# An earlier weight order, a later sum of squares and a second issuer of outputs in a three-layer kernel

## The chip, the cores and the metric

The kernel runs on one core of a Trainium2 chip. The metric is the device time of one execution in microseconds (us), given as the median of several runs. The core has five engines that matter here: TensorE (PE, with its weight loads shown apart as PEld), VectorE (DVE), ScalarE (ACT), GpSimd (POOL) and SyncE (SP), which mostly issues transfers. Each engine takes its instructions in the order in which the program holds them, and semaphores make one wait for another.

## The reference

512 tokens of 1024 features go through three layers in fp32. Each layer starts with an rms norm, whose scale per token is `rsqrt(mean(x*x) + 1e-6)`. The change touches the start of the first layer and the very end.

```python
def rmsnorm(x, g):
    return x * lax.rsqrt(jnp.mean(x * x, axis=-1, keepdims=True) + EPS) * g

def even_mixer(h, w_in, sink, w_pool, pool_scale, w_out):
    z = h @ w_in                                   # q, k, v and u side by side
    q, k, v, u = jnp.split(z, [...], axis=-1)
    q, k = rope(q), rope(k)
    ya = windowed_gqa(q, k, v, sink)               # 8 heads, 2 key heads, |i-j| <= 128
    yb = multiscale_pool(u, w_pool, pool_scale)    # centred means over 2, 4, 8, 16 tokens
    return jnp.concatenate([ya, yb], axis=-1) @ w_out

x = x + even_mixer(rmsnorm(x, g0), ...);  x = x + sq_relu_mlp(rmsnorm(x, g1), ...)
x = x + odd_mixer(rmsnorm(x, g2), ...);   x = x + sq_relu_mlp(rmsnorm(x, g3), ...)
...                                        # a third mixer and a gated embedding
return rmsnorm(x, norm_final)
```

## The kernel before

Every matrix product is computed as three products of two-part numbers: an operand is split into a high part of fewer bits and a low remainder, and hi·wh, hi·wl and lo·wh are added up in PSUM. So each piece of a weight (`wr`, as it comes from memory) needs a `wh` (a rounding copy) and a `wl` (`wr` minus `wh`) before TensorE can use it, and each of the 8 chunks of the transposed activations `x` (128 features by 512 tokens) needs a `hi` and a `lo`. In the first norm the gain is folded into `hi` and `lo`; the scale per token (`rb`) is multiplied in after the first matrix product, so that product can start before the norm is known.

The first tile of the program is the weight unit `ein2`, 8 pieces of 128x256 (k = 0 to 7), by the 8 chunks of `x`: for each k six matmuls of 512 columns, 48 in all, into two PSUM tiles. Then come the units `ein0`, `ein1` and so on in pieces of 128x1024. From the eight chunks also come the squares for the norm: `sq<-x` squares a chunk, `sq<-sq,sq` adds two partial sums, and when all eight are in one tile four matmuls by a column of ones (`tr<-onec,sq`) sum them over features. From there the chain is `ms` (DVE), `pw` (POOL, the power), `tr<-cst,pw` (PE, which spreads the scale over partitions), `rb<-tr` (a DVE copy), and then the rotary tables `cst<-cst,rb`. Every q and k head needs these tables: a raw product is copied to `zs`, turned on PE (`tr<-zs`), combined by `ra` and `rbb`, split into `q` or `kh` and `kl`, and only then do the scores `sc`, their maxima `mx`, the probabilities `p`, their turned halves `ph` and `pl` and the products `av` follow, head after head. Between these stand matmuls of other units that need no norm; they are what keeps TensorE at work while the other engines do the attention.

Where an instruction stands, and on which engine, is set while the program is built: a planner keeps a clock (`fl.now`) and an estimate of when each engine is free (`_Engine.cost`), steps a list of generators, and lets `first` choose the engine that would be done first. Constants of that choice stand in the table `_TUNE`, one row for each phase: `gw` is added to the estimate of POOL for weight splits, `gt` for adds, `gc` for copies, so a larger number keeps that work off POOL. A generator that waits for another (`waitc`) is passed over until the other is planned. So a small edit in the front re-orders everything up to the point at which the plans fall together again. For the first layer's mixer the row is "a". The outputs are written at the end by `outputs`: a PSUM tile is scaled by ACT or DVE (again by `first`) and written to memory by a DMA that SP issues.

Of the kernel before, what the change touches and what calls it, by code (L numbers as in the profile page):

```python
# [18 lines left out]
P = 128  # L19
T = 512  # L20
# [220 lines left out]
def _constants():  # L241
# [40 lines left out]
    for dl in (4, 16):  # L282
# [16 lines left out]


_TUNE = {
    "a": dict(slack=2, gc=0.3, gt=-0.6, gw=-0.5, low=1, lat=0.1, wide=1, mm=4, sc=2, tr=5, av=2, ahead=3,
              streams=3, share=0.1),
    "b": dict(slack=0.5, gc=0.4, gt=0, gw=0, low=4, lat=0.15, wide=2, mm=4, sc=4, tr=4, av=2),
# [63 lines left out]
class _Flow:  # L368
# [12 lines left out]
    def go(self, gen, low=False):  # L381
        t = _Task(gen, low)
        t.due = self.now + 0.1
        self.tasks.append(t)
        return t
# [103 lines left out]
def tile_hybrid(ctx: ExitStack, tc: tile.TileContext, wt, xT, pT, prm_d, cst_d, out):  # L489
    nc = tc.nc  # L490
# [3 lines left out]
    fl = _Flow()  # L494
    go = fl.go
    V, S, G = (_Engine(fl, e, k) for e, k in ((nc.vector, "V"), (nc.scalar, "S"), (nc.gpsimd, "G")))
# [13 lines left out]
    def uid(s):  # L510
        cnt[0] += 1
        return f"{s}{cnt[0]}"

    def blk(name="b", dt=F32, n=T):
        return bp.tile([P, TB], dt, tag="b", bufs=NB, name=uid(name))[:, 0:n]
# [17 lines left out]
    def take(tag):  # L533
        while (t := bank(tag)) is None:
            yield
        return t
# [6 lines left out]
    def give(tag):  # L543
        banks.append(max(fl.now, fl.last) + 0.1)
        held[tag] -= 1

    def wait(*tasks):
        for t in tasks:
            while not t.done:
                yield  # L550

    def waitc(*tasks):
        for t in tasks:
            while not t.done:
                yield 0.1
# [15 lines left out]
    def first(*engines):  # L571

        return min(engines, key=lambda e: max(e[0].free, fl.now) + e[1])[0]
# [28 lines left out]
    units, order = {}, []  # L602
# [160 lines left out]
    x, x_at = [], []  # L763
    for c in range(NC):

        x.append(blk("x"))
        (nc.scalar if c == 0 else nc.sync).dma_start(x[c], xT[:, c, :])
        wl["dma"] = max(wl["dma"], fl.now) + 0.73
        x_at.append(wl["dma"] + 2.0)
        order[c // 4].load()  # L770
        if c == 0:
            nc.sync.dma_start(prm, prm_d)
    cst = cons.tile([P, NKEEP], F32, name="cst")
# [11 lines left out]
    def PR(name, i=0, n=1):  # L785
        o, w = _PO[name]
        return prm[:, o + i:o + i + n]
# [55 lines left out]
    def mm3(ps, w, c, a, start, stop, m=P, bw=P, cs=slice(0, T), keep=False):  # L843

        us = 0.216 * (cs.stop - cs.start) / T
        wh, wlo = yield from w.at(c, bw, keep)
        mm(ps, wh[:, :m], a.hi[:, cs], start, False, us)
        mm(ps, wlo[:, :m], a.hi[:, cs], False, False, us)
        mm(ps, wh[:, :m], a.lo[:, cs], False, stop, us)
        yield  # L850
# [86 lines left out]
    def v_stack(z):  # L937

        ps = yield from takec("tr")
        for b in range(NQ):  # L940
            tr(ps[:, b * P:(b + 1) * P], z[:, b * P:(b + 1) * P], ident)
        r = []
        yield
        for i in range(2):
            v = blk("v", F32R).rearrange("p (b h t e) -> p b h t e", b=2, h=2, t=2)
            src = ps[:, 256 * i:256 * i + 256].rearrange("p (b h e) -> p b h e", b=2, h=2)
            copy(v[:, :, :, 0, :], src)
            r.append((v, src))
        yield
        for v, src in r:  # L950
            V.tensor_sub(v[:, :, :, 1, :], src, f(v[:, :, :, 0, :]))
        give("tr")
        yield
        return lambda kb, h: r[kb // 2][0][:, kb % 2, h, :, :]
# [12 lines left out]
    def k_stacks(z, dst, i=0):  # L967

        ks = [(blk("kh", F32R), blk("kl", F32R)) for _ in range(2)]
        for r0, (kh, kl) in zip((0, 64), ks):  # L970
            copy(kh[r0:r0 + 64], z[r0:r0 + 64])
            copy(kh[64 - r0:128 - r0], z[r0:r0 + 64])
        yield
        for r0, (kh, kl) in zip((0, 64), ks):
            V.tensor_sub(kl[r0:r0 + 64], z[r0:r0 + 64], f(kh[r0:r0 + 64]))
            V.tensor_sub(kl[64 - r0:128 - r0], z[r0:r0 + 64], f(kh[r0:r0 + 64]))
        yield
        dst[i], dst[i + 1] = ks
# [162 lines left out]
    def attend(jobs, ahead=2, streams=1):  # L1141

        n = [0, 0]

        def scores():
            for ready, score, _ in jobs:
                while n[0] - n[1] >= ahead or (ready is not None and not ready()):
                    yield
                yield from score()
                n[0] += 1  # L1150

        def applies(k):
            for i in range(k, len(jobs), streams):
                while n[0] <= i:
                    yield
                yield from jobs[i][2]()
                n[1] += 1

        return _both(*[applies(k) for k in range(streams)], scores())
# [69 lines left out]
    h = acts()  # L1229

    def start(c):
        while fl.now < x_at[c]:
            yield 0.1
        yield from split_to(h[c], x[c], PR("e_norm", c))

    def sums():
        for c in range(NC):
            yield from waitc(h[c])
            go(ss.add(x[c]))

    for c in range(NC):
        go(start(c))
    go(sums())
    r_t, rb = rms(ss)
    cosr, sinr = C("cos64"), C("sin64")
# [22 lines left out]
    def rope64(ps, then):  # L1268

        zs = blk("zs")  # L1270
        S.activation(zs, ps, AF.Copy)
        give("mm")
        yield
        yield from waitc(rp)
        ps2 = yield from takec("tr")
        mm(ps2, C("perm"), zs, True, True, 0.86)
        a, b_ = blk("ra"), blk("rbb")
        tt(ALU.mult, a, zs, cosr)
        yield
        V.tensor_mul(b_, ps2, sinr)  # L1280
        give("tr")
        tt(ALU.add, a, a, b_)
        yield
        yield from then(a)
# [12 lines left out]
    def kv_blocks():  # L1297
        w = weights("ein2")
        kps = yield from take("mm")
        ps = yield from take("mm")  # L1300
        for k in range(NC):
            yield from wait(h[k])
            for b, o in enumerate((kps, ps)):
                yield from mm3(o, w, (2 * k + b) * P, h[k], k == 0, k == NC - 1)
        go(rope64(kps, lambda z: k_stacks(z, ks)))

        def vchain(ps=ps):
            yield from waitc(rb)
            z = blk("vz")
            V.tensor_mul(z, ps, rb.t)  # L1310
            give("mm")
            yield
            v0.append((yield from v_stack(z)))

        go(vchain())
# [57 lines left out]
    def store(hd, base, post=None):  # L1373

        def done(po):
            i = hd // 2
            if i not in yz:
                yz[i] = [blk("ya"), 0]
            y = yz[i][0]
            yield from combine(po, y[64 * (hd % 2):64 * (hd % 2) + 64])  # L1380
            yz[i][1] += 1
            if yz[i][1] == 2:
                del yz[i]
                if post is not None:
                    yield from post(i, y)
                yield from split_to(yhl[base + i], y)
        return done

    def job0(hd):
        st = {}  # L1390

        def score():
            g = hd // 4
            q = qs[hd]
            st["h"] = Head([(q, ks[g][0]), (q, ks[g][1])], band3, band3_masks, lambda kb: v0[0](kb, g),
                           SC64, nsink=nsink[:, hd:hd + 1], sink=PR("sink", hd))
            return st["h"].score()

        return (lambda: hd in qs and 1 in ks and v0 and nmask.done, score,
                lambda: st["h"].apply(done=store(hd, 4)))  # L1400

    fl.phase("a")
    fl.run(kv_blocks(), None)
    fl.run(attend([job0(i) for i in range(8)], fl.ahead, fl.streams), fill, fl.share)
    ss = SumSq(NC)
    h, then = next_norm(lambda c: PR("n_mlp0", c), (ss, None))
# [98 lines left out]
    h = h2  # L1505
# [276 lines left out]
    h, then = next_norm(lambda c: PR("n_mlp1", c), (ss, None))  # L1782
# [15 lines left out]
    h = h2  # L1798
# [73 lines left out]
    gt = cons.tile([P, 18, NQ], F32, name="gt")  # L1872
# [480 lines left out]
    def outputs(t, b, j, r, tag):  # L2353

        yield from waitc(dense)
        ps = yield from takec(tag)
        for i in range(4):
            z = xg[NC * t + 4 * j + i]
            yield from waitc(z)
            tr(ps[:, i * P:(i + 1) * P], z.t[:, 256 * t + b * P:256 * t + (b + 1) * P], ident)  # L2360
        yield
        yield from waitc(r)
        o = blk("o")
        if first((S, 0.53), (V, 0.6)) is S:
            S.activation(o, ps, AF.Copy, scale=r.t[:, b:b + 1])
        else:
            V.tensor_scalar(o, ps, r.t[:, b:b + 1], None, op0=ALU.mult)
        give(tag)
        q = 256 * t + P * b
        nc.sync.dma_start(out[q:q + P, T * j:T * j + T], o)  # L2370
        yield

    fl.phase("e")
# [13 lines left out]
    h = h2  # L2387
# [26 lines left out]
```

## Time and profile before

| what | value |
|---|---|
| median of 3 runs | 1486.02 us (1485.08 to 1486.47) |
| the profiled execution, its own time | 1481.19 us |
| its span, first to last instruction | 1479.4 us |
| mean granted TensorE clock | 0.993 |
| PE busy | 1450.2 us, 98% of the span |
| DVE busy | 906.4 us, 61% |
| ACT busy | 639.5 us, 43% |
| POOL busy | 328.3 us, 22% |

The durations of the section on rows belong to the profiled execution, which ran 4.8 us below the median. In the rows, a name such as `wl<-wr,wh` tells the tile written and the tiles read, with buffer numbers left out; `128x512` is partitions by elements. What stands in square brackets is how long the engine had been idle before the row, and what ended that wait. The mixer that this change re-orders lies in the first 160 us of the span. Matmuls of 512 columns follow each other every 0.23 us although each shows about 0.39, since they are pipelined.

### The profile page before, as it was taken

What the parts mean: (1) busy time and instruction counts of PE and PEld (TensorE: products, weight loads), DVE (VectorE), ACT (ScalarE), POOL (GpSimd) and SP (SyncE); (2) the same over time, 40 slices, a digit from 0 to 9 for tenths busy, and PEclk for the clock granted to TensorE, in tenths of its full rate; (3) what the DMA queues carried; (4) which work ended last, traced back from release to release, by engine and by line L of the source; (5) the groups of instructions that cost most, each with busy time, mean ns of one, the idle gap of its engine ahead of it and who ended that gap; (6) DMA issues with size and microseconds to landing.
All of it is one profiled execution on the core that took longest, in us unless ns stands there. A gap on an engine that the chain in (4) does not pass through costs nothing.

```text
span 1479.4 us, 18899 instructions
## 1 busy us (share of the span) xinstructions
PE 1450.2 (98%) x6789; PEld 1175.9 (79%) x6789; DVE 906.4 (61%) x1414; ACT 639.5 (43%) x1175; POOL 328.3 (22%) x307
## 2 busy tenths in 40 slices
PE   8999999999999999799999999999999999999998
PEld 5777878888888887688888888888887788888787
DVE  7896865646434458987675665756755566536413
ACT  5684433323223345477343433334521575324623
POOL 5441220202102026542120210202110000110332
PEclk9999999999999999899999999999999999999999
DMA  6113688898333363331599999999855323346352
GB/s 220 44 43 100 209 276 284 284 290 283 108 100 101 141 221 130 127 129 72 188 312 332 334 325 331 320 334 320 305 204 201 114 86 115 114 174 216 109 196 88
DMA packets 118317, 291.44 MB, mean 197 GB/s; under 512 B 13136, under 2 KB 14672, under 8 KB 118224
## 3 DMA queue, kind: packets, MB, share of 16 engines
q1 hardware_dynamic: 118080, 289.98, 57.7%
q8 instruction: 53, 0.87, 0.2%
q14 instruction: 40, 0.33, 0.1%
q10 hardware_dynamic: 144, 0.26, 0.1%
HBM read 205.26 MB, written 84.93 MB: 196 GB/s over the span
## 4 chain that ended last, share of the span: by engine, by line
PE 90%; DVE 5%; DMA 2%; ACT 1%; issue 1%; POOL 0%; SPq 0%; POOLq 0%; DVEq 0%; ACTq 0%
PE mm L561 78%; PE sc L561 4%; PE tr L565 3%; PE av L561 3%; DVE sg L363 2%; PE tr L561 1%; DMA kr<-in_wt_dram 1%; DVE lo L363 1%; DVE wl L363 1%; DMA pin<-in_pT_dram 0%; DMA x<-in_xT_dram 0%; ACT wh L363 0%; DMA wk<-khi 0%; ACT sg L363 0%; POOL ma L363 0%
## 5 line engine op out<-in xcount | busy, mean ns | idle before, releaser
L561 PE MATMUL mm<-hi,wh 128*128 128x512 f32 (+1 forms) x1276 | 508.4, 398 | 0.8 <-POOL wh L363 0.5
L561 PE MATMUL mm<-hi,wl 128*128 128x512 f32 (+1 forms) x1276 | 502.1, 393 | 4.8 <-DVE wl L363 2.7
L561 PE MATMUL mm<-lo,wh 128*128 128x512 f32 (+1 forms) x1276 | 500.2, 392 | 0.3 <-POOL lo L363 0.3
L561 PEld LDWEIGHTS mm<-hi,wl 128*128 128x128 f32 x1276 | 241.0, 189 | 56.1 <-DVE wl L363 4.2
L561 PEld LDWEIGHTS mm<-lo,wh 128*128 128x128 f32 x1276 | 240.9, 189 | 55.3 <-POOL lo L363 0.8
L561 PEld LDWEIGHTS mm<-hi,wh 128*128 128x128 f32 x1276 | 241.2, 189 | 53.0 <-issue 1.1
L363 ACT ACTIVATE khi<-kr 128x512 fp32r<-128x512 f32 x120 | 75.9, 632 | 304.6 <-DMA kr<-in_wt_dram 298.3
L561 PE MATMUL mm<-ul,wh 128*128 128x512 f32 x512 | 201.6, 394 | 0.3 <-DVE ul L363 0.3
L561 PE MATMUL mm<-uh,wh 128*128 128x512 f32 x512 | 201.6, 394 | 0.0
L561 PE MATMUL mm<-uh,wl 128*128 128x512 f32 x512 | 201.5, 394 | 0.0
L363 DVE TENSOR_TENSOR wl<-wr,wh 128x1024 fp32r<-128x1024 f32 (+1 forms) x145 | 182.9, 1262 | 6.2 <-ACT wh L363 5.6
L363 DVE TENSOR_TENSOR klo<-kr,khi 128x512 fp32r<-128x512 f32 x150 | 121.4, 810 | 81.8 <-ACT khi L363 73.1
L363 ACT ACTIVATE wh<-wr 128x1024 fp32r<-128x1024 f32 (+1 forms) x147 | 148.8, 1013 | 47.6 <-PE mm L561 34.4
L363 DVE TENSOR_TENSOR x<-x,mm 128x512 f32<-128x512 f32 x112 | 76.8, 686 | 147.1 <-PE mm L561 143.7
L363 POOL TENSOR_TENSOR ma<-ma 128x512 f32<-128x512 f32 x62 | 86.6, 1397 | 279.3 <-ACT uh L363 237.6
L561 PEld LDWEIGHTS mm<-ul,wh 128*128 128x128 f32 x512 | 96.1, 188 | 23.8 <-DVE ul L363 1.3
L561 PEld LDWEIGHTS mm<-uh,wl 128*128 128x128 f32 x512 | 96.2, 188 | 22.3
L561 PEld LDWEIGHTS mm<-uh,wh 128*128 128x128 f32 x512 | 96.1, 188 | 22.3
L363 ACT ACTIVATE p<-sc,nm 128x512 f32<-128x512 f32 (+3 forms) x136 | 75.3, 557 | 27.8 <-DVE nm L363 24.8
L363 POOL TENSOR_SCALAR khi<-kr 128x512 fp32r<-128x512 f32 x30 | 29.6, 986 | 248.1 <-DMA kr<-in_wt_dram 225.8
L363 DVE TENSOR_TENSOR pl<-tr,ph 128x512 fp32r<-128x512 f32 (+2 forms) x108 | 66.3, 624 | 27.9 <-ACT ph L363 27.1
L363 DVE SCALAR_TENSOR_TENSOR ma<-mm,rb 128x512 f32<-128x512 f32 x64 | 44.1, 690 | 59.0 <-PE mm L561 58.9
(293 smaller groups left out, 1633.4 us busy)
## 6 DMA issues: line engine op xcount, KB each, us to landing
wr<-in_wt_dram SPq DMA_DIRECT2D x144, 512.0 KB, 5.2
kr<-in_wt_dram SPq DMA_DIRECT2D x150, 256.0 KB, 5.8
wk<-khi SPq DMA_DIRECT2D x150, 256.0 KB, 5.9
wk<-klo SPq DMA_DIRECT2D x150, 256.0 KB, 5.7
wh<-wk SPq DMA_DIRECT2D x74, 512.0 KB, 3.3
wl<-wk SPq DMA_DIRECT2D x74, 512.0 KB, 4.2
x<-xs SPq DMA_DIRECT2D x16, 256.0 KB, 5.0
cst<-in_cst_dram SPq DMA_DIRECT2D x8, 256.0 KB, 5.1
```

The costliest lines, as they stand in the source:

```text
L363: return fn(*a, **k)
L561: PE.matmul(o, l, r, start=start, stop=stop, skip_group_check=True)
L565: PE.transpose(o, i, idn)
```

## The change

There are four edits. The weight piece of `ein2` is asked for ahead of the chunk of `x` of the same k, not behind it. A new phase "s", with 3 us put on POOL for weight splits and adds, holds while the first tile is planned; phase "a" begins behind it. The generator of the sums (`sums`) starts only when all eight splits of `x` are planned, and adds one chunk at each step. In `outputs`, the engine that issues a DMA is ACT where ACT has scaled the tile, and SP otherwise.

```diff
 _TUNE = {
+    "s": dict(slack=2, gc=0.3, gt=3, gw=3, low=1, lat=0.1, wide=1, mm=4, sc=2, tr=5, av=2),
     "a": dict(slack=2, gc=0.3, gt=-0.6, gw=-0.5, low=1, lat=0.1, wide=1, mm=4, sc=2, tr=5, av=2, ahead=3,
...
     for c in range(NC):
+        order[c // 4].load()
         x.append(blk("x"))
         (nc.scalar if c == 0 else nc.sync).dma_start(x[c], xT[:, c, :])
...
-        order[c // 4].load()
...
     def sums():
+        yield from waitc(*h)
         for c in range(NC):
-            yield from waitc(h[c])
             go(ss.add(x[c]))
-
+            yield
+
+    fl.phase("s")
     for c in range(NC):
         go(start(c))
     go(sums())
...
+    fl.run(kv_blocks(), None)
     fl.phase("a")
-    fl.run(kv_blocks(), None)
     fl.run(attend([job0(i) for i in range(8)], fl.ahead, fl.streams), fill, fl.share)
...
-        if first((S, 0.53), (V, 0.6)) is S:
+        e = first((S, 0.53), (V, 0.6))
+        if e is S:
             S.activation(o, ps, AF.Copy, scale=r.t[:, b:b + 1])
...
-        nc.sync.dma_start(out[q:q + P, T * j:T * j + T], o)
+        (nc.scalar if e is S else nc.sync).dma_start(out[q:q + P, T * j:T * j + T], o)
```

TensorE's instructions are the same in kind and number, 6704 matmuls. From the 608th matmul on they stand in the same order in both programs; ahead of that all engines are re-ordered.

POOL from its first work on, in the program before. `wl` and `wh` are the halves of weight pieces, `sq` the squares and their sums.

```order
L363 TENSOR_TENSOR wl_141<-wr_77,wh_140 128x256 x2
L363 TENSOR_TENSOR sq_148<-sq_148,sq_163 128x512
L363 TENSOR_TENSOR wl_141<-wr_77,wh_140 128x256
L363 TENSOR_TENSOR wl_185<-wr_91,wh_184 128x256
L363 TENSOR_SCALAR wh_140<-wr_77 128x256
L363 TENSOR_TENSOR sq_187<-sq_187,sq_177 128x512
L363 TENSOR_TENSOR sq_194<-sq_194,sq_187 128x512
L363 TENSOR_TENSOR wl_185<-wr_91,wh_184 128x256 x2
L363 TENSOR_TENSOR sq_241<-sq_241,sq_194 128x512
```

POOL at the same place in the changed program.

```order
L364 TENSOR_SCALAR wh_137<-wr_75 128x256
L364 TENSOR_SCALAR wh_181<-wr_89 128x256 x2
L364 TENSOR_TENSOR sq_228<-x_77 128x512
L364 TENSOR_TENSOR sq_238<-x_87 128x512
L364 TENSOR_TENSOR sq_247<-x_91 128x512
L364 TENSOR_TENSOR sq_254<-sq_254,sq_256 128x512
L364 TENSOR_TENSOR pw_349<-ms_344,nhalf 128x4
L364 TENSOR_TENSOR wl_364<-wr_259,wh_363 128x512
```

The low halves `wl` of the first tile have gone from POOL to DVE, two more of the one-operand splits `wh` have come to POOL, and the squares of three chunks of `x`, each a product of two operands, now stand there behind them; they wait for nothing but their chunk. Names carry buffer numbers in such listings: `wr_75` and `wr_89` hold pieces of `ein2`, four each.

On ACT the splits `wh` of k = 6 and k = 7 stand, in both programs, one ahead of and one behind the split of the first piece of `ein0`, with one square between that piece and k = 7. On DVE the low half of k = 7 now stands behind the low half of that piece of `ein0` and one sum of squares.

PE where the squares are summed, before. `mm_277` is the first tile of `ein0`.

```order
L561 MATMUL mm_277<-hi_137,wh_233 128x512
L561 MATMUL mm_277<-hi_137,wl_234 128x512
L561 MATMUL mm_277<-lo_138,wh_233 128x512
L561 MATMUL tr_281<-onec,sq_241 128x1 x4
L561 MATMUL mm_277<-hi_145,wh_233 128x512
L561 MATMUL mm_277<-hi_145,wl_234 128x512
L561 MATMUL mm_277<-lo_146,wh_233 128x512
```

The same place in the changed program, where `mm_311` is the second tile, that of `ein1`.

```order
L562 MATMUL mm_311<-hi_177,wh_244 128x512
L562 MATMUL mm_311<-hi_177,wl_245 128x512
L562 MATMUL mm_311<-lo_178,wh_244 128x512
L562 MATMUL tr_336<-onec,sq_254 128x1 x4
L562 MATMUL mm_311<-hi_190,wh_244 128x512
L562 MATMUL mm_311<-hi_190,wl_245 128x512
L562 MATMUL mm_311<-lo_191,wh_244 128x512
```

The four matmuls that sum the squares stood behind 51 matmuls of the products and now stand behind 87. In both programs 12 more follow before the scale is spread (`tr<-cst,pw`): 63 stood ahead of that, and 99 do now. The first scores stood behind 117 and now stand behind 150, the last `av` of the heads behind 294 and now 348. On DVE, between the copy `rb<-tr` and the last `pl`, stood two residual adds `x<-x,mm` and eight splits `wl`; now eight adds and nine splits stand there.

ACT at the end of the program, before, from the last `sg` on (a sigmoid of the gate).

```order
L363 ACTIVATE sg_13348<-mm_13279 128x256
L363 ACTIVATE o_13353<-sc_13322,pw_13295 128x512
L363 ACTIVATE o_13373<-sc_13359,pw_13295 128x512
L363 ACTIVATE sq_13376<-x_12417 128x256
L363 ACTIVATE o_13387<-av_13334,pw_13385 128x512
L363 ACTIVATE o_13393<-mm_13344,pw_13385 128x512
```

The same in the changed program.

```order
L364 ACTIVATE sg_13348<-mm_13279 128x256
L364 ACTIVATE o_13353<-sc_13322,pw_13295 128x512
L2374 DMA out_dram<-o_13353 128x512
L364 ACTIVATE o_13373<-sc_13359,pw_13295 128x512
L2374 DMA out_dram<-o_13373 128x512
L364 ACTIVATE sq_13376<-x_12417 128x256
L364 ACTIVATE o_13387<-av_13334,pw_13385 128x512
L2374 DMA out_dram<-o_13387 128x512
L364 ACTIVATE o_13393<-mm_13344,pw_13385 128x512
L2374 DMA out_dram<-o_13393 128x512
```

Four of the eight output DMAs now stand in ACT's queue, each behind the scaling that it writes out, and two of them ahead of the last `sq`. The other four stay on SP.

## Rows read from the trace of the kernel before

**Rows 1.** Page, busy us of each engine, share of the span, instructions.

```profile
PE 1450.2 (98%) x6789; PEld 1175.9 (79%) x6789; DVE 906.4 (61%) x1414; ACT 639.5 (43%) x1175; POOL 328.3 (22%) x307
```

**Rows 2.** Waits of PE, 0 to 170 us: total us, times, longest us.

```profile
PE mm L561 <- DVE wl L363: 2.7, 3, 1.4
PE av L561 <- DVE pl L363: 2.3, 2, 1.9
PE mm L561 <- POOL wl L363: 2.0, 3, 1.1
```

**Rows 3.** Timeline of PE, 5 to 24 us: start us, us, instruction, idle before.

```profile
5.73 0.50 PE L561 MATMUL mm<-hi,wh 128*128 128x512 f32 x1 [0.19 <-ACT wh L363]
...
15.86 0.40 PE L561 MATMUL mm<-lo,wh 128*128 128x512 f32 x1
16.09 0.39 PE L561 MATMUL mm<-hi,wh 128*128 128x512 f32 x1
...
22.76 0.39 PE L561 MATMUL mm<-hi,wh 128*128 128x512 f32 x1
...
23.45 0.72 PE L561 MATMUL tr<-onec,sq 128*128 128x1 f32 x6
```

**Rows 4.** Timeline of DVE, 4 to 24 us.

```profile
13.97 1.49 DVE L363 TENSOR_TENSOR wl<-wr,wh 128x256 fp32r<-128x256 f32 x1
...
18.24 0.41 DVE L363 TENSOR_TENSOR wl<-wr,wh 128x256 fp32r<-128x256 f32 x1
```

**Rows 5.** Timeline of POOL, 4 to 24 us.

```profile
12.68 0.84 POOL L363 TENSOR_SCALAR wh<-wr 128x256 fp32r<-128x256 f32 x1
13.48 3.13 POOL L363 TENSOR_TENSOR sq<-sq,sq 128x512 f32<-128x512 f32 x2
```

**Rows 6.** Timeline of ACT, 4 to 24 us.

```profile
16.86 1.06 ACT L363 ACTIVATE wh<-wr 128x1024 fp32r<-128x1024 f32 x1 [0.97 <-DMA wr<-in_wt_dram]
...
18.35 1.35 ACT L363 ACTIVATE wh<-wr 128x256 fp32r<-128x256 f32 x2
```

**Rows 7.** Timeline of DVE at the scale's copy and at the last `pl`.

```profile
27.75 0.69 DVE L363 COPY rb<-tr 128x512 f32<-128x512 f32 x1 [2.01 <-PE tr L565]
...
120.71 0.56 DVE L363 TENSOR_TENSOR pl<-tr,ph 128x384 fp32r<-128x384 f32 x1 [0.28 <-ACT ph L363]
```

**Rows 8.** Two windows: us, busy us (count) of PE, PEld, DVE, ACT, POOL.

```profile
27.75:121.00 93.25, 88.79 (x466) 71.09 (x465) 83.59 (x171) 65.83 (x157) 42.01 (x46) 1.00 0.19 60
86.00:112.43 26.43, 22.00 (x124) 17.45 (x124) 24.25 (x57) 23.58 (x59) 14.86 (x15) 1.00 0.16 48
```

**Rows 9.** DVE's groups from 28.0 to 121.8 us: count, busy us, mean ns.

```profile
L363 DVE TENSOR_TENSOR wl<-wr,wh 128x1024 fp32r<-128x1024 f32 x8 | 12.8, 1595 | 0.8 <-ACT wh L363 0.6
...
L363 DVE TENSOR_TENSOR kl<-ra,kh 64x512 fp32r<-64x512 f32 x4 | 5.1, 1263 | 0.0
...
L363 DVE TENSOR_TENSOR x<-x,mm 128x512 f32<-128x512 f32 x3 | 2.0, 681 | 1.1 <-PE mm L561 1.1
```

**Rows 10.** Timelines: PE at the last `av`, DVE with one undisturbed split.

```profile
122.03 0.28 PE L561 MATMUL av<-pl,v 128*128 128x256 f32 x1
...
117.19 1.22 DVE L363 TENSOR_TENSOR wl<-wr,wh 128x1024 fp32r<-128x1024 f32 x1
```

**Rows 11.** A window; the third number from the right is the granted clock.

```profile
575.00:578.00 3.00, 3.00 (x9) 2.32 (x8) 1.83 (x2) 3.00 (x7) 2.75 (x3) 0.50 0.00 0
```

**Rows 12.** Timeline of the end.

```profile
1469.38 6.83 SPq L2370 DMA_DIRECT2D out_dram<-o  x8
...
1471.04 0.69 ACT L363 ACTIVATE o<-sc,pw 128x512 f32<-128x512 f32 x1 [1.33 <-PE sc L565]
...
1471.62 0.41 ACT L363 ACTIVATE sq<-x 128x256 f32<-128x256 f32 x1
1472.08 0.52 PEld L561 LDWEIGHTS tr<-onec,sq 128*128 128x128 f32 x4 [0.59 <-ACT sq L363]
```

**Rows 13.** Timeline of the start: the DMA that ACT issues.

```profile
0.72 0.41 ACTq L767 DMA_DIRECT2D x<-in_xT_dram  x1
```

## Prediction, made before the changed kernel ran

> **What bounds the kernel now.** I read the page's busy shares first: PE is busy for 1450.2 us, 98% of the span [rows 1], and has the same matmuls in both programs, so time can only be won or lost where PE waits. The second view is PE's waits in the first 170 us, the only stretch that is re-ordered apart from the very end: 2.7 us in three waits for `wl` of DVE, 2.0 us in three for `wl` of POOL, 2.3 us in two for `pl` of DVE [rows 2]. Third come the timelines, which tell two places apart.
>
> The first tile: 48 matmuls go out from 5.73 to 22.76 us, 17.0 us [rows 3]. At the pitch of two following rows, 16.09 - 15.86 = 0.23 us [rows 3], they need 11.1. So 5.9 us is lost here, and this is what the change aims at.
>
> The attention of the first mixer: from the copy of the scale at 27.75 us to the last `pl`, which ends at 120.71 + 0.56 = 121.3 us [rows 7]. DVE is busy for 83.59 of the 93.25 us up to 121 [rows 8]. It is nearly as full there as PE and stands in front of it: from 86.00 to 112.43 us PE is busy for only 22.00 of 26.43, 4.4 us lost [rows 8].
>
> Why operations of DVE stretch matters for both. The low half of a 128x256 piece took 0.41 us when POOL was idle, and 1.49 us when POOL was at a sum of squares from 13.48 on [rows 4, 5]. All operands of both lie in SBUF. The same shows in the groups of the attention: `kl` of 512 columns took 1.263 us on average, while the adds of 512 columns, which read PSUM, took 0.681 [rows 9]; the eight splits of 1024 columns took 1.595 against 1.22 for one undisturbed [rows 9, 10].
>
> The Trainium skill, SBUF — State Buffer, Who interferes with whom, has it as a rule: a DVE instruction with two inputs in SBUF and any GpSimd instruction that reads SBUF shut each other out for a whole instruction. The stretched rows agree [rows 4, 5]. The rule speaks against half of this change, since a split with one operand or a square of `x` on POOL reads SBUF too; a first tile free of all collisions would gain about 2.4 us, and by the rule it keeps some and gains less. The bound for that comes from the queues in the next part.
>
> **The change part by part.** The profiled execution took 1481.2 us, with 1.8 us around its span; the median is 4.8 us above it. I work out a difference on the profile and put it on the median.
>
> 1. The order of weight and chunk in memory shifts each by one transfer of 128 KB, a few tenths of a us in opposite directions. PE's waits there are for `wl` and `wh`, not for DMAs [rows 2], and the last piece is not what the tile waits for, as the next term shows. Zero.
>
> 2. The first tile. The last piece, k = 7, decides. Its `wh` stands on ACT behind the first piece of `ein0`, whose split cannot start before its data, at 16.86 us [rows 6]; before, this split of k = 7 went out at 18.35 [rows 6], and nothing in front of it has changed. PE, without any wait for k = 0 to 6, would be there at 5.73 + 42 x 0.23 = 15.4 us, so waits earlier in the tile no longer count. The `wl` of k = 7 is now on DVE, behind the low half of that piece of `ein0` (1.22 us, from about 17.9) and one sum of squares (0.6): it starts at 19.7, ends at 20.15, and five matmuls of the tile follow. The tile ends at about 21.4 against 22.76: **-1.4 us**. If DVE had nothing in front, it would end at 20.4, -2.4 us; if the split collides with POOL once more, as the one that took 1.49 [rows 4], about 1.1 us of this goes. So -2.4 to -0.3.
>
> 3. The squares. They are summed on PE behind 87 matmuls and no longer behind 51, so 36 x 0.232 = 8.35 us later in PE's own order, less 1.4 of the tile: the scale's copy moves from 27.75 [rows 7] to about 34.7 us, **6.95 us later**. Nothing of the attention can start before it. PE does not notice at once, since the matmuls moved ahead cover it: this work is what PE did later between the heads. DVE has little to do from about 28 to 34.
>
> 4. The attention, where it ends. DVE's last `pl` ended at 121.3 [rows 7]. It starts 6.95 later, and has six more residual adds in front (6 x 0.61 = 3.7, 0.68 less an overlap of 0.07) and one more split of 1024 columns (1.1): 121.3 + 6.95 + 4.8 = 133.0 us, with collisions and idle time as before. On PE the last `av` started at 122.03 [rows 10] and has 54 matmuls more in front, 12.5 us; with the tile's -1.4, and if every us of the 4.4 lost before [rows 8] went, PE would be there at 122.0 + 12.5 - 1.4 - 4.4 = 128.7. So even then it waits 4.3 + 0.2 = 4.5 us in all, as long as before.
> What collisions and idle time become I worked out by laying the two queues beside each other, instruction by instruction, with the durations of rows such as those in [rows 4, 5, 9] and one rule: of a DVE instruction with two SBUF inputs and one of POOL that reads SBUF, the later waits. In the program before this gives 7 us of collisions in the attention, and in the changed one 12: POOL takes a second split of 1024 columns and two parts of `lo`, and `q`, `den` and a pooling sum of DVE now fall behind such rows. DVE's idle time grows by 4, most of it where it waits for scores and turned probabilities that stand behind more matmuls on PE. So the last `pl` ends at 133.0 + 4.7 + 4.0 = 141.7, and PE waits 141.7 + 0.2 - 128.7 = 13.2 us instead of 4.4: **+8.8 us**. The bounds: +0.1 with collisions and idle time as before, +10.8 with 2 us more of them; a gain of 4.4 if DVE's 9.7 us of idle time [rows 8] took half of the delay. I take the upper value because most of what DVE idles for is in the chain itself (PE's `sc`, ACT's `q`) and moves with it. From the 608th matmul on the order is the same, and PE has hardly another wait to give the time back.
>
> 5. The outputs. The second DMA of ACT stands between the scaling at 1471.04 and the last `sq` at 1471.62 [rows 12]; a DMA issue of ACT took 0.41 us [rows 13]. PE's last sum waits for that `sq` [rows 12], so the last norm comes up to 0.5 us later. In return SP's last issues no longer follow each other at 0.4: eight went out over 6.83 us [rows 12]. Between -0.2 and +0.5, I take **+0.2**.
>
> The Trainium skill, DMA: Bandwidth & Descriptors, Issuing engines are not separate DMA queues, says that several issuers save only the time of the issue itself, since all transfers share the same engines. By that rule the end gains a few tenths at most, and no run so far shows it.
>
> Sum: -1.4 + 8.8 + 0.2 = **+7.6 us**; on the profile 1488.8, on the median 1486.0 + 7.5 = **1493.5**.
>
> **The rivals.** DVE's idle time takes the delay (the other side). If DVE, held up by 6.95 us, works off its queue without its 9.7 us of idle time [rows 8], the last `pl` is there by 128.5, PE never waits, and 1.4 + 4.4 - 0.2 = 5.6 us is won: 1480.4. For it speaks that the order gives PE matmuls enough; against it that DVE had no idle time for which a chain was not the reason. It decides from 131 on: a last `pl` earlier than that makes the kernel faster by over 3 us. Chance 0.12.
>
> No new collisions. Idle time and collisions stay as they were: -1.4 + 0.1 + 0.2 = -1.1, 1484.9. For it: before, the collisions came to only about 5 us by the long rows [rows 9]. Chance 0.17.
>
> The clock. Behind waits of PE the granted clock was 0.50 for a stretch of 3 us [rows 11], so 1.5 us of work was lost. If the new waits bring one such stretch on top, 1495. For it: the waits come close together. Against it: after the 1.4 and the 1.9 us of [rows 2] it did not fall. Chance 0.10.
>
> The change does not do what it says. POOL's squares of `x` wait only for their chunk, so they run in the middle of the first tile and block the `wl`, as before; the tile gains nothing and the rest is lost, 1495. Chance 0.08.
>
> **How the numbers follow.** My forecast has 0.53. A measurement of this kernel can tell about 0.2%, 3.0 us, from no change. Slower by more: 0.53 + 0.10 + 0.08 = 0.71; within: 0.17; faster: 0.12. The range goes from 1484.5, which takes in the case without new collisions, to 1497.5, the forecast with 2 us more of collisions and the clock; the gain of 5.6 us lies outside.
>
> **What would show it.** First tile: the first matmul of `ein0` at 21.4 us and a wait for `wl` at k = 7. The scale's copy at 34.7. PE's waits between 60 and 145 us at 13 us in place of 4.4, for `wl`, `pl` and `lo`, and DVE rows of `q` or `den` three times as long as before. The last `av` at about 142. At the end `sq` half a us later behind its `o`. The prediction is wrong if the last `pl` comes before 131, or if the waits after 60 us stay under 5.

## The result, and the profile after

The change made the kernel slower: 1498.79 us (median of 6 runs, 1493.65 to 1501.63) against 1484.63 (6 runs), a ratio of 1.0088 (95% interval 1.0069 to 1.0107), so 10 to 16 us. Run again beside other kernels on another occasion it was 1492.96 us against 1484.32, 1.0057 (1.0042 to 1.0072), 6 to 11 us. The prediction had said 1493.5, within 1484.5 to 1497.5.

The profiled execution of the changed kernel has a span of 1496.9 us, 17.5 above that of before. Of this some 3.4 us come with the choice of executions: the profiled one of before, 1481.19 us, lies that much below the median of its six runs, the one of the change, 1498.66, at its median. Page, busy shares:

```profile
PE 1456.9 (97%) x6786; PEld 1176.1 (79%) x6789; DVE 915.2 (61%) x1424; ACT 640.2 (43%) x1173; POOL 323.0 (22%) x299
```

The program has the same matmuls as before, and yet PE is busy for 6.7 us more than in [rows 1]: part of the loss does not show as waiting. (The row of a matmul of 512 columns lasts 0.39 us and the next starts 0.23 us behind it [rows 3], so a pause of under 0.16 us counts as busy.) Two windows of the changed kernel (length, PE, PEld, DVE, ACT, POOL busy; the third number from the right is the granted clock), up to the sum of the second norm and from there to that of the third, and then two short ones:

```profile
5.00:176.84 171.84, 154.95 (x728) 118.92 (x728) 138.09 (x242) 99.40 (x210) 55.92 (x52) 0.99 0.31 97
176.84:538.91 362.07, 359.99 (x1553) 291.32 (x1552) 188.45 (x251) 112.24 (x147) 56.52 (x44) 1.00 0.65 209
...
79.00:82.00 3.00, 3.00 (x10) 2.37 (x9) 1.65 (x4) 3.00 (x8) 0.56 (x3) 0.54 0.00 0
226.00:229.00 3.00, 3.00 (x8) 2.30 (x7) 1.34 (x2) 0.00 (x0) 0.00 (x0) 0.50 1.01 371
```

The same two stretches of the kernel before:

```profile
5.00:163.58 158.58, 149.84 (x729) 118.85 (x728) 130.85 (x232) 99.86 (x213) 60.76 (x60) 1.00 0.32 106
163.58:521.79 358.21, 357.90 (x1552) 290.17 (x1551) 188.99 (x251) 111.95 (x146) 56.53 (x44) 1.00 0.65 211
```

The first norm and mixer have become 13.3 us longer, of which PE's waits (length less busy) are 16.9 - 8.7 = 8.2 and longer work on the same matmuls 5.1; the first MLP 3.9 us longer, of which waits 1.8 and work 2.1. Twice the granted clock stood at half, the lower of its two levels, for 3.4 us (from 79.2 and from 226.0 us), each time after waits close together, which costs 1.7 us of work each time. From the third norm on nothing has changed until the outputs, where 0.7 us are lost. 13.3 + 3.9 + 0.7, less 0.3 between, is 17.5 but for rounding.

Waits of PE from 24 to 165 us (total, times, longest us), of the kernel before and then of the changed one:

```profile
PE av L561 <- DVE pl L363: 2.3, 2, 1.9
PE mm L561 <- DVE wl L363: 1.2, 2, 0.6
PE av L561 <- ACT ph L363: 0.4, 1, 0.4
PE mm L561 <- POOL lo L363: 0.3, 1, 0.3
```

```profile
PE mm L562 <- ACT hi L364: 2.8, 3, 1.5
PE av L562 <- DVE pl L364: 2.2, 5, 0.6
PE tr L566 <- ACT p L364: 1.6, 2, 0.9
PE mm L562 <- DVE wl L364: 1.5, 2, 0.9
PE mm L562 <- POOL lo L364: 1.3, 2, 0.6
PE mm L562 <- DVE lo L364: 1.1, 2, 0.8
PE mm L562 <- POOL wl L364: 0.8, 1, 0.8
```

There are 17 waits in place of six, for work of three engines, none over 1.5 us: no single thing is late. Timeline of DVE of the changed kernel at the scale's copy and the last `pl`:

```profile
37.14 0.69 DVE L364 COPY rb<-tr 128x512 f32<-128x512 f32 x1 [3.17 <-PE tr L566]
...
147.65 0.54 DVE L364 TENSOR_TENSOR pl<-tr,ph 128x384 fp32r<-128x384 f32 x1
```

DVE's groups of the kernel before from 28.0 to 121.8 us, and of the changed one from 36.9 to 149 us (count, busy us, mean ns):

```profile
L363 DVE TENSOR_TENSOR den<-den,es 128x4 f32<-128x4 f32 x8 | 1.3, 156 | 0.9 <-ACT es L363 0.8
...
L363 DVE TENSOR_TENSOR us<-up 128x527 f32<-128x527 f32 x1 | 0.7, 708 | 0.1
```

```profile
L364 DVE TENSOR_TENSOR q<-ra,q 64x512 fp32r<-64x512 f32 x8 | 7.3, 912 | 0.2
...
L364 DVE TENSOR_TENSOR den<-den,es 128x4 f32<-128x4 f32 x8 | 3.9, 486 | 1.5 <-ACT es L364 1.5
...
L364 DVE TENSOR_TENSOR us<-up 128x527 f32<-128x527 f32 x1 | 2.8, 2822 | 0.0
```

Against [rows 7] the copy comes 9.4 us and the last `pl` 26.9 us later, with 12.5 us of matmuls moved ahead of the last `av`. `den`, four elements a row, took 0.49 us on average in place of 0.16, and one sum of the pooling (`us`) 2.8 in place of 0.7: DVE stood behind POOL. Three of the eight `den` overlap a row of POOL and took 0.63, 1.22 and 1.25 us, and so does the `us`; the other five overlap none and took at most 0.16. Not all went this way: `kl` took 0.87 us and had taken 1.26 [rows 9].

The first tile, timelines of PE, POOL and ACT of the changed kernel:

```profile
16.89 0.50 PE L562 MATMUL mm<-hi,wl 128*128 128x512 f32 x1 [1.58 <-DVE wl L364]
...
21.15 0.50 PE L562 MATMUL mm<-hi,wh 128*128 128x512 f32 x1 [1.47 <-ACT wh L364]
...
22.52 0.50 PE L562 MATMUL mm<-hi,wl 128*128 128x512 f32 x1 [0.87 <-DVE wl L364]
...
11.86 4.10 POOL L364 TENSOR_TENSOR sq<-x 128x512 f32<-128x512 f32 x3
...
19.21 1.06 ACT L364 ACTIVATE wh<-wr 128x1024 fp32r<-128x1024 f32 x1 [4.28 <-DMA wr<-in_wt_dram]
```

POOL's three squares run in the middle of the tile, and PE waits 1.58 us for a `wl` that DVE could not do meanwhile (two `lo` in front of it took 2.97 us, at 0.75 for one undisturbed). That wait did not move the end of the tile, since PE then had to wait for k = 7 all the same. The piece k = 7 waits for ACT, which waits 4.28 us for the first piece of `ein0`, as the prediction describes; in this execution its data came at 19.2 and not at 16.9 us [rows 6]. The next tile begins at 23.78 (22.76 in [rows 3]). In the second profile of the same program (e9 below) it begins at 21.99, with that data at 17.4.

The end: ACT, its DMA issue and PE's weight load of the changed kernel.

```profile
1487.87 0.69 ACT L364 ACTIVATE o<-sc,pw 128x512 f32<-128x512 f32 x1 [1.32 <-PE sc L566]
1488.59 0.34 ACTq L2374 DMA_DIRECT2D out_dram<-o  x1
1488.98 0.42 ACT L364 ACTIVATE sq<-x 128x256 f32<-128x256 f32 x1 [0.41 <-ACT o L364]
...
1489.45 0.52 PEld L562 LDWEIGHTS tr<-onec,sq 128*128 128x128 f32 x4 [1.12 <-ACT sq L364]
```

The last `sq` starts 1.11 us behind the start of the scaling, not 0.58 as in [rows 12]. All fourteen profiles of this document agree: in the six with this edit the `sq` starts 1.1 us behind, and the span ends 15.1 to 15.2 us behind PE's last sum but one of the `sq`; in the eight without it 0.6, and 14.4 to 14.5. So this edit by itself costs 0.6 to 0.7 us.

### The profile page after: what moved, and what is told of

It reads as the page before. It is cut to its first block, busy times and chain, and to the rows that moved or that the text cites. A ratio compares the mean times of both kernels' runs of the same rounds, so it can differ in the third digit from the quotient of the medians.

```text
span 1496.9 us, 18888 instructions
## 1 busy us (share of the span) xinstructions
PE 1456.9 (97%) x6786; PEld 1176.1 (79%) x6789; DVE 915.2 (61%) x1424; ACT 640.2 (43%) x1173; POOL 323.0 (22%) x299
## 4 chain that ended last, share of the span: by engine, by line
PE 86%; DVE 7%; DMA 3%; ACT 2%; issue 1%; POOL 1%; SPq 0%; POOLq 0%; ACTq 0%; DVEq 0%
PE mm L562 74%; PE sc L562 4%; PE tr L566 3%; PE av L562 3%; DVE sg L364 2%; DMA kr<-in_wt_dram 1%; PE tr L562 1%; DVE wl L364 1%; DMA x<-in_xT_dram 1%; DVE mx L364 1%; DMA wr<-in_wt_dram 1%; DVE lo L364 1%; ACT p L364 0%; DMA wk<-khi 0%; DMA pin<-in_pT_dram 0%
## 5 line engine op out<-in xcount | busy, mean ns | idle before, releaser
L364 ACT ACTIVATE wh<-wr 128x1024 fp32r<-128x1024 f32 (+2 forms) x144 | 147.2, 1022 | 47.8 <-PE mm L562 34.4
L364 ACT ACTIVATE p<-sc,nm 128x512 f32<-128x512 f32 (+3 forms) x136 | 75.4, 558 | 36.0 <-DVE nm L364 27.8
```

The costliest lines, as they stand in the source:

```text
L364: return fn(*a, **k)
```

## Experiments

The theories. A, that of the prediction: the norm's sum stands later on PE, so the attention starts later and a full DVE cannot make up for it. B: the first tile, by the order of transfers and the splits on DVE. C: any edit of the front makes the planner draw the whole attention anew, and what a plan costs depends on how the engines' queues happen to mesh in it, not on the edit. D and E: whether PE, in such a plan, waits for a DVE that has too much to do, or for chains whatever DVE's load.

**The edits apart.** e1 makes only the edit of `sums()`, e2 the other three, e3 only the order of transfers, e4 only the issuer of the outputs.

> Only the edit of sums() is made, on the kernel before. The squares are then summed on PE behind 99 matmuls (51 before, 87 in the whole change), the last av of the heads stands behind 348 (294). Theory A, the late norm sum delays the attention and DVE cannot catch up: slower by 9 to 16 us, with the rb copy at 37 to 40 us and PE waits of 10 us or more between 60 and 150 us. Theory B, the first tile (order of transfers, splits on DVE) is what costs: within 3 us of before.

> The whole change without the edit of sums(). The squares are summed behind 63 matmuls, the last av stands behind 288. Theory A: within 4 us of before, with the rb copy at 30 to 33 us. Theory B: slower by 9 us or more, as the whole change.

> Only the order of the transfers is changed, weight piece ahead of the chunk of x. The planner then sums the squares behind 45 matmuls. Theory A: between -2 and +2 us. Theory B: slower by 2 us or more, with the first matmul half a us later (6.2 in place of 5.7) and the first piece of ein0 landing 2 us later (19 in place of 16.8), as in the changed kernel.

> Only the issuer of the output DMAs is changed; everything ahead of the last 10 us is the same program. Both theories: +0.2 to +0.7 us, from the last sq standing 0.4 to 0.5 us later behind ACT's second DMA issue; span from the last sq to the end as before.

```diff
 # e1, on the kernel before
     def sums():
+        yield from waitc(*h)
         for c in range(NC):
-            yield from waitc(h[c])
             go(ss.add(x[c]))
+            yield
 # e2: the change, with these lines taken back
 # e3, on the kernel before
+        order[c // 4].load()
         x.append(blk("x"))
...
-        order[c // 4].load()
 # e4, on the kernel before
-        nc.sync.dma_start(out[q:q + P, T * j:T * j + T], o)
+        (nc.scalar if e is S else nc.sync).dma_start(out[q:q + P, T * j:T * j + T], o)
```

Each of the first three costs as much as all together did in e9: 1.0064 (1.0042 to 1.0086), 1.0069 (1.0047 to 1.0091) and 1.0061 (1.0041 to 1.0082). (The first measurement of the whole change, 1.0088, lies 0.3% above e9's 1.0057 for the same program, so differences of that size between occasions tell nothing about a plan.) The time of e4 is that of the kernel before within what can be told, 1.0002 (0.9988 to 1.0017); its profile shows the 0.6 us at the end. For e1 theory A had the time right, with the copy at 35.6 us, a little ahead of what it asked for; but A falls with e3: there the sum stands behind 45 matmuls, earlier than before, and the kernel is as slow. It falls with e2 too, whose copy came at 32.2 as A asked, and which is slower by 10 us in place of under 4. B, as the only cause, falls with e1, which has the old transfers, and whose first tile is faster by 4.4 us (the next tile begins at 18.32), while its mixer is slower by far more. The signs of B in e3 failed as well: its first matmul came at 5.9 us and its first piece of `ein0` at 17.15, so a landing at 19 does not belong to the order of the transfers.

**How late the sum is, and plans drawn anew without any of the edits.** e5 lets `sums()` wait for all `h` but keeps the adds together. e6 has only the phase "s". e7 and e8 change one constant of the planner's row "a" and nothing else.

> On the kernel before, sums() waits for all eight h, but adds the squares without a yield between them. The norm's sum stands behind 90 matmuls, as late as in the changed kernel (87), but the last av stands behind 306 (before 294, changed 348). Theory A, the late norm sum is the cause: slower by 9 us or more. Theory C, what counts is how the attention's instructions mesh after the plan is drawn anew, and before's plan meshes well: by laying the queues beside each other with the durations of the trace, only about 2 us more of PE waits up to the second norm, so +1 to +5 us.

> Only the phase s is added on the kernel before: no low half of a weight and no sum on POOL in the first tile. The norm's sum stands behind 42 matmuls (earlier than before's 51), the last av behind 294. Theory A: between -2 and +2 us. Theory C: about 2 us more of PE waits in the attention, so +1 to +5 us, more where the clock falls after them.

> None of the four edits; the planner's guess lat of phase a is 0.12 in place of 0.10, which draws the plan anew. The norm's sum stands behind 60 matmuls, the last av behind 312. Theory A: +0 to +3 us (9 matmuls are 2.1 us). Theory C: 5 us more of PE waits in the attention plus clock drops behind them, +5 to +11 us.

> None of the four edits; the planner's constant gc of phase a (copies on POOL) is 0 in place of 0.3, which draws the plan anew: the norm's sum behind 54, the last av behind 288. Theory C with the laid out queues: as good as before, within 3 us. A theory that every new plan is some 10 us worse than before's expects +8 us or more.

```diff
 # e5, on the kernel before
-            yield from waitc(h[c])
+            yield from waitc(h[max(c, 7)])
 # e6: the row "s", fl.phase("s") ahead of the first tile and fl.phase("a") behind it
 # e7
-    "a": dict(slack=2, gc=0.3, gt=-0.6, gw=-0.5, low=1, lat=0.1, ...
+    "a": dict(slack=2, gc=0.3, gt=-0.6, gw=-0.5, low=1, lat=0.12, ...
 # e8
+    "a": dict(slack=2, gc=0, gt=-0.6, gw=-0.5, low=1, lat=0.1, ...
```

e5, with the sum as late as in the change, costs only 1.0033 (1.0018 to 1.0048); e6, with the sum earlier than before, 1.0025 (1.0013 to 1.0037). e7 and e8, which contain none of the edits, cost 1.0048 (1.0033 to 1.0063) and 1.0062 (1.0046 to 1.0078). So these two plans drawn anew are slower by 7 to 9 us though nothing is edited. This much of C is shown: a new plan alone can cost what the change costs. That the first three edits cost nothing by themselves is not shown. e8 was a miss of mine: laid out in queues, its plan was as good as before's, and on the chip PE waited 14.5 us up to the second norm. Its time is the one asked for by the other theory named there, that every new plan is some 10 us worse; against that one stand e5 and e6, with 4 to 5 us. How a plan will mesh could be told from durations only to some 5 to 10 us.

**The change under another plan, and with less work for DVE.** e9 is the change again; e10 the change with one constant of the planner altered; e11 the change, and e12 the kernel before, with the same order of all instructions, but with maxima that read every fourth column, which leaves out three quarters of the scores in the offset of the softmax and takes some 8 us from DVE.

> The changed kernel once more, on the chip of the next three, as the mark for them. +12 to +16 us against before; the first piece of ein0 landing at 19 us again if that belongs to the order of the transfers, at about 17 if it was this one execution.

> The whole change, all four edits, with the planner's constant gc of phase a at 0.15 in place of 0.3: the norm's sum stands behind 87 matmuls as in the change, the attention is planned anew. If the edits themselves cost the time (late sum, transfers, splits): +12 to +16 us as the change. If it is how the plan meshes (theory C): the laid out queues give about 5 us less of PE waits than for the change, so +4 to +10 us.

> The changed kernel with the same order on all engines, but the 32 maxima mx of the first mixer read only every fourth column of the scores, so DVE has about 8 us less to do in the attention; the softmax is then computed with another offset. Theory D, PE waits for a full DVE: the waits in the attention fall from 11 us to 5 or less, and the kernel is 5 to 9 us faster than the change. Theory E, PE waits for chains over several engines whatever DVE's load: within 3 us of the change.

> The kernel before with the same short maxima and the same order. Theory D: PE's 4.4 us of waits in the attention shrink to 1 or 2, 2 to 4 us faster than before. Theory E: within 2 us of before.

```diff
 # e10, on the changed kernel
-    "a": dict(slack=2, gc=0.3, gt=-0.6, ...
+    "a": dict(slack=2, gc=0.15, gt=-0.6, ...
 # e11 on the changed kernel, e12 on the one before
-                    V.reduce_max(mx, ps[:, o:o + n], axis=AX.X)
+                    V.free = max(V.free, fl.now) + V.cost("reduce_max", (mx, ps[:, o:o + n]), dict())
+                    fl.last = max(fl.last, V.free)
+                    nc.vector.reduce_max(mx, ps[:, o:o + n:4], axis=AX.X)
```

Up to the second norm (5 us to its sum; the columns as above), e9:

```profile
5.00:174.75 169.75, 154.82 (x728) 118.86 (x727) 137.37 (x239) 97.67 (x206) 54.84 (x52) 0.99 0.30 98
```

e10:

```profile
5.00:167.21 162.21, 151.84 (x728) 119.43 (x727) 132.31 (x242) 95.09 (x201) 58.89 (x60) 0.99 0.31 103
```

e11:

```profile
5.00:169.49 164.49, 154.33 (x730) 119.35 (x729) 130.68 (x241) 98.39 (x210) 54.79 (x52) 0.99 0.31 102
```

e9 cost 8.6 us, not the 12 to 16 expected, with the first piece of `ein0` at 17.4. e10 has all four edits and the sum behind 87 matmuls like the change; it passes the second norm 7.5 us earlier than e9 with 4.6 us less of waits, and takes 1490.43 us, 1.0041 (1.0028 to 1.0055), against 1.0057 for e9. Their intervals overlap, so the times do not part them. The profiles do for the attention: from the end of the first tile to the second norm PE waited 7.0 us in e10 and 11.3 and 11.4 in the two executions of the change; 2.3 us of the gain are lost again in the first MLP. Windows of that stretch, e9 and e10:

```profile
21.99:174.75 152.76, 141.41 (x679) 110.28 (x678) 123.48 (x221) 86.57 (x188) 49.60 (x46) 0.99 0.23 74
```

```profile
21.84:167.21 145.37, 138.39 (x679) 110.89 (x678) 118.23 (x223) 83.94 (x183) 53.10 (x54) 0.99 0.24 78
```

e11 takes 1488.76 us, 1.0029 (1.0017 to 1.0041), 4 us less than e9: PE's waits fell by 4.8 us for 8 us less of work on DVE, 6.7 by its busy time. Theory D has about half of it, less than the 5 to 9 us that it asked for: part of the waits come from a full DVE. The rest stayed: `tr<-cst,p` waits longer for ACT's `p` than in the change (2.1 us in 24 to 165, where that had 1.6). And e12, with 7 us less of work for DVE, takes the time of the kernel before, 0.9997 (0.9986 to 1.0009): in that plan DVE's load cost nothing that can be measured.

All of it side by side; the waits are length less PE's busy time from 5 us to the second norm's sum, and the clock is the mean granted one of that stretch:

| kernel | sum behind | last `av` behind | second norm at | PE waits up to it | clock up to it | ratio |
|---|---|---|---|---|---|---|
| before | 51 | 294 | 163.6 | 8.7 | 1.00 | 1 |
| the change | 87 | 348 | 176.8 | 16.9 | 0.99 | 1.0088 |
| e9, the same | 87 | 348 | 174.8 | 14.9 | 0.99 | 1.0057 |
| e1 | 99 | 348 | 174.6 | 12.9 | 0.95 | 1.0064 |
| e2 | 63 | 288 | 174.5 | 13.2 | 0.96 | 1.0069 |
| e3 | 45 | 300 | 174.3 | 13.2 | 0.97 | 1.0061 |
| e4 | 51 | 294 | 164.7 | 7.9 | 0.99 | 1.0002 |
| e5 | 90 | 306 | 170.5 | 10.6 | 0.97 | 1.0033 |
| e6 | 42 | 294 | 168.8 | 10.3 | 0.98 | 1.0025 |
| e7 | 60 | 312 | 171.8 | 13.4 | 0.97 | 1.0048 |
| e8 | 54 | 288 | 173.5 | 14.5 | 0.97 | 1.0062 |
| e10 | 87 | 342 | 167.2 | 10.4 | 0.99 | 1.0041 |

Neither column of positions orders the times. In time, the copy of the scale came later than before's 27.8 us in every plan drawn anew, so that a part of the loss comes with that is not excluded; but the losses do not grow with it (e3 at 30.1 and e8 at 31.4 lost 9 us each, e5 at 34.7 lost 5, e10 at 35.2 lost 6). Of the ten plans here, that of before is the best.

The waits are not the whole delay. e1 passes the second norm 11.0 us later than before with 4.2 us more of waits; the other 6.8 are longer work on the same matmuls, at a mean granted clock of 0.95. In e2 and e3 it is 6.5 of 11.0 and 6.2 of 10.7, at 0.96 and 0.97. Windows of e1, up to the second norm and at its longest fall of the clock there, which begins as a wait of 3.1 us ends:

```profile
5.00:174.55 169.55, 156.63 (x730) 123.45 (x728) 137.96 (x235) 97.06 (x206) 60.76 (x59) 0.95 0.30 98
66.20:76.40 10.20, 8.64 (x21) 5.79 (x22) 8.17 (x24) 7.84 (x23) 3.45 (x5) 0.50 0.15 51
```

So a plan costs its waits and longer work besides; in e1, e2 and e3 the second part is the larger.

**The first MLP.** Its instructions stand in the same order in both programs, yet it lost 3.9 us (e9: 1.5). Timelines of ACT and PE of the changed kernel:

```profile
182.79 0.64 ACT L364 ACTIVATE khi<-kr 128x512 fp32r<-128x512 f32 x1 [4.84 <-DMA kr<-in_wt_dram]
...
220.46 0.64 ACT L364 ACTIVATE khi<-kr 128x512 fp32r<-128x512 f32 x1 [4.46 <-DMA kr<-in_wt_dram]
221.00 1.04 ACT L364 ACTIVATE wh<-wr 128x1024 fp32r<-128x1024 f32 x1
221.94 0.62 ACT L364 ACTIVATE uh<-ma 128x512 fp32r<-128x512 f32 x1
...
224.98 0.51 PE L562 MATMUL mm<-ul,wh 128*128 128x512 f32 x1 [1.63 <-DVE ul L364]
```

ACT's queue holds the splits of later weights (`khi<-kr`) ahead of the `uh` that PE needs, and each waits for its transfer. The split at 220.46 came 43.6 us behind the second norm's sum; before, the same one started at 205.08, 41.5 us behind it. So the transfers came 2 us later against PE, and `uh` and then `ul` came late; before, PE waited 0.3 us at this place. e5 and e6, which reached the second norm earliest of the edited plans apart from e10, show no such wait; e10 does, so the delay alone is not the reason.

The traces show most of the way back. Timelines of DVE and POOL, of the kernel before and then of the changed one:

```profile
171.97 0.68 DVE L363 TENSOR_TENSOR klo<-kr,khi 128x512 fp32r<-128x512 f32 x1
172.13 1.43 POOL L363 TENSOR_TENSOR ma<-ma 128x512 f32<-128x512 f32 x1 [5.30 <-ACT uh L363]
```

```profile
185.54 1.54 DVE L364 TENSOR_TENSOR klo<-kr,khi 128x512 fp32r<-128x512 f32 x1
185.49 1.04 POOL L364 TENSOR_TENSOR ma<-ma 128x512 f32<-128x512 f32 x1 [5.40 <-ACT uh L364]
```

Before, DVE's `klo` began ahead of POOL's `ma` and took 0.68 us; in the change it began 0.05 us behind it and took 1.54. The `wl` that stands behind this `klo` ended 1.4 us later against the second norm, and SP's next weight transfer, which waits for that `wl` and stands ahead of the later transfers, went out 12.6 us behind the second norm in place of 11.2. The fourteen profiles fall in two groups: five with a `klo` of 0.68 us and that transfer at 11.2 to 11.3 (before, e4, e5, e6, e12), in which PE waited at most 0.3 us in the first MLP, 1.1 in e12; and nine with a `klo` of 1.54 or 1.55 and the transfer at 12.6 to 13.7, in which it waited 1.5 to 3.2. In the nine, the transfer for which ACT waited 4.84 us above had its split start 6.0 to 7.0 us behind the second norm, in the five 5.0 to 5.8. Why it landed later was not tried on the chip.

## Why the prediction was wrong, point by point

What bounds the kernel (PE, with the attention's DVE close behind) and the direction were right. The sum was 7.6 us; 14.2 were measured between the medians, and 8.6 in e9, with the size at fault in four terms. Against -1.4 + 8.8 + 0.2 the profile of the change shows +1.0 for the first tile, +12.2 for the attention up to the second norm, +3.9 for the first MLP, which stood at nothing, and +0.7 for the outputs, less 0.3 between; that of e9 shows -0.8, +11.9, +1.5 and +0.7. That e9's median came within about 1 us of the forecast is luck: its profile shows 11.9 and 1.5 where the forecast had 8.8 and nothing. The step that failed in both is the attention (3 and 4): the late sum was made the cause of what a redrawn plan costs by itself, and the cost was priced by PE's waits alone, with the longer work that came with them put at nothing. The two signs of being wrong that the prediction named did not come (the last `pl` before 131 us; the waits after 60 us under 5, where 10.6 were measured to 145); they guarded the direction, not the size. Two of its sums are off by a little: 1486.0 + 7.6 is 1493.6, and the forecast with 2 us more and the clock's 1.5 is 1497.0, not 1497.5.

The first tile, step 2: -1.4 predicted, +1.0 in the profile of the changed kernel, -0.8 in that of e9. That k = 7 decides, behind the first piece of `ein0` on ACT and DVE, was right. What was mis-sized is the landing of that piece: I took 16.9 us from one execution as fixed, and two executions of the changed program had 19.2 and 17.4.

The later sum, step 3: the copy of the scale came at 37.1 in place of 34.7, 2.4 later, which is the tile again. But its role failed. I made the late sum the reason why the attention loses time; e3, e6, e7 and e8 lose 4 to 9 us with the sum within 9 matmuls of before or ahead of it, and e5 and e10 lose 5 and 6 with the sum as late as in the change. What these have in common is that the plan is another one. I had seen that everything up to the 608th matmul is re-ordered and still looked for one delay that runs through it.

The attention, step 4: 13.2 us of PE waits in place of 4.4 predicted, 11.4 in place of 4.5 measured. The last `pl`, forecast to end at 141.7 us, ended at 148.2, of which the tile is 2.4. The two queues laid side by side did tell which rows would be stretched (`q` 0.91, `den` 0.49, `us` 2.8 us). What was missing is what waits cost besides themselves. Windows from the end of the first tile to the second norm, before and changed:

```profile
22.76:163.58 140.82, 136.36 (x679) 109.99 (x678) 115.58 (x218) 85.21 (x187) 47.19 (x49) 1.00 0.25 80
```

```profile
23.78:176.84 153.06, 141.69 (x680) 110.35 (x679) 123.96 (x223) 87.75 (x191) 50.43 (x46) 0.99 0.24 74
```

The same matmuls kept PE busy for 5.3 us longer. Of these 1.7 come from one fall of the clock, which I had only as a rival. Some 1.1 come from restarts, an estimate: a matmul behind a wait is followed after 0.33 us and not 0.23 (16.89 to 17.22 and 17.22 to 17.45 in the changed kernel), and there are 17 such waits in place of six. What makes up the other 2.5 is open.

"PE has hardly another wait to give the time back": wrong by 3.9 us, since later waits could grow. The place where PE waited 0.3 us before had no margin, and I read only that there was no slack to win. Behind the 608th matmul the order is the same but not the timing: a shift of 0.2 us between DVE's `klo` and POOL's `ma` decided which of them stood in front.

The outputs, step 5: +0.2 taken, within -0.2 to +0.5; +0.7 measured in the profile of the change. The second issue on ACT holds up `sq` as described; the end in return gained nothing. All six profiles with this edit show it; e4 shows that it is too little to be measured in the time.

The base: the profile of before was an execution without a fall of the clock in the attention. e4 and e12, with the same order up to the outputs (e12 with the short maxima), each had one at 113 us, e4 behind the same wait of 1.9 us. Timeline of PE and a window of e4:

```profile
111.70 0.44 PE L561 MATMUL av<-pl,v 128*128 128x384 f32 x1 [1.91 <-DVE pl L363]
```

```profile
113.00:116.00 3.00, 3.00 (x10) 2.43 (x9) 2.00 (x5) 2.35 (x5) 1.64 (x2) 0.50 0.54 190
```

I had argued against the clock as a rival with this very wait, since nothing had followed it in one execution.

The rule of the Trainium skill (SBUF — State Buffer, Who interferes with whom) that was set against the change agrees with the rows: while the squares ran on POOL, 4.10 us in the middle of the first tile, a `wl` of DVE took 1.26 us in place of 0.42 and two `lo` 2.97 in place of twice 0.75. What the Trainium skill says in DMA: Bandwidth & Descriptors, Issuing engines are not separate DMA queues, agrees with e4, where a second issuer gained nothing at the end.

## What to carry to other kernels

Where a planner fixes the order from estimates, a measured version is one draw of many, and may be a good one, as here the best of ten. A local edit throws it away, and the new draw can cost time by itself (7 to 9 us here, with a constant of the planner changed and no edit at all). Before reading an edit's effect, time a few neutral draws; or keep the order outside the edit fixed. And price a wait of the full engine with its restart and a possible fall of its clock, not by its length alone.

## What the runs showed of the hardware

The granted clock fell to half behind waits that were each short (0.6 to 1.5 us, five of them between 67 and 78 us in the changed kernel), and behind one wait of 1.9 us in one execution (e4) and not in another of the same order (before). Nine waits of 0.3 to 0.9 us between 98 and 115 us of the changed kernel were followed by no fall. Each of the changed kernel's two falls lasted 3.4 us, which is 1.7 us of work; one in e1, at the end of a wait of 3.1 us, lasted 10.2 us.

A DVE subtraction of 512 columns from SBUF (`klo`) took 0.68 us where it began ahead of a POOL operation, and 1.54 where it began 0.05 us behind the same one (before and the change).

The first transfers of the kernel differ between executions of one program: the split of the first large piece could start at 19.2 and 17.4 us in two executions of the change, and at 16.86, 16.30 and 18.55 in three whose front is that of before (before, e4, e12).
